# A hybrid attention and DeltaNet backbone: the emission order waits for small transfers, row loads move into the last column block, and scale-and-shift steps choose their engine

## The chip, the core and the metric

The kernel runs on one core of a Trainium2 chip. The metric is the device time of one execution in microseconds: 1731.31 us, the median of three runs (1731.27 to 1731.7). The engines are TensorE (PE in the profile; its weight loads are PEld), VectorE (DVE), ScalarE (ACT), GpSimd (POOL) and SyncE (SP), which issues nearly all transfers.

## What is computed

Two layers act on 256 latent tokens and 256 context tokens of width 2048. Per layer and stream:

```
h  = layernorm(x) * (1 + scale) + shift          # scale, shift, gate = silu(c) @ w_mod + b_mod
p  = h @ w_in                                    # 2048 x 6672: q, k, v, gates of three head groups
ya = attention(qa, ka, va) * silu(za)            # group A: 8 query heads on 2 key heads; rmsnorm and rotary on q, k
yb = window_attention(qb, kb, vb, bias) * silu(zb)   # group B: 4 heads, learned 2-D bias
yc = rmsnorm(gated_deltanet(conv(qkv))) * silu(zc)   # group C: 4 heads, forward and backward scans over chunks
y  = concat(ya, yb, yc) @ w_out                  # 2048 x 2048
x  = layernorm(ALPHA * x + gate * y) * ln_g + ln_b
```

Latent tokens also attend to the context's keys, and the scans start from the context's states. In the second layer the context serves only keys, values and states; its queries, gates and output are left out, so those items of `w_in` run on the latent columns alone. The output is the latent stream.

## The kernel before

**Tiling.** Everything is fp32. Activations lie transposed (features on the partitions) in 16 tiles of 128 features, 512 tokens wide (context in columns 0 to 255). Each fp32 product is three matmuls in a reduced format: the weight and the activation are each split into a high and a low part (`wHL` from `raw`; `hH`, `hL` or `hv`). Splitting a weight piece of 128x512 costs a copy (`high`, on ScalarE or VectorE) and a subtraction on VectorE. One item of `w_in` makes 128 output features and is four such pieces, accumulated in one PSUM bank of ring `mm` (two banks). The output projection goes by column blocks `nb` of 512 and over 16 feature tiles `k` in `K_ORDER`; `ki` counts them.

**Order of the work.** The program plans its own instruction order (class `Order`, L102). It keeps an estimated time for each engine; every emitted operation moves its engine's time on by a cost formula, and a transfer is taken to land 2.0 us after its issue (0.75 us on SP, 1.0 on POOL). Side work is written as Python generators, the tasks. A task yields when it would have to wait; `poll` (L185), called between matmuls, resumes those whose time has come on PE's estimated clock and stops when VectorE or ScalarE are planned 2.5 or 3.5 us ahead of PE. A plain `yield` waits until what the task has issued so far should be done, `yield 0` until the next poll, and `yield ("at", t)` until the planned time t. `until` (L201) moves PE's planned time forward until a condition holds. The engines then run each its own instructions strictly in this order, and wait for real semaphores.

**Buffers.** A `Ring` (L215) hands out the buffers of one size: `tmp` has five, `cin` fifteen, `yq` eighteen, `wr` sixteen; `get` waits for one to be free at the planned time.

**The pieces that the change touches.** `mod_dve` (L650) computes part of the second layer's modulation on VectorE, beside the first layer's projections: eight times it broadcasts 256 values to a tile `xsb` by two transfers on SP, then multiplies rows with it. `ln_scale` gives mean and scale of rows; `normalise` (L753) applies them to a 128x512 piece, by turns on ScalarE and VectorE. `h_run` (L786) transposes the normalised rows and applies scale and shift, by turns too. `gates` (L885) prepares the scan's decays. `ev_ka` (L1003) and `ev_qa` (L1050) take a key or query projection out of PSUM, with squares `sq`, the rotary's temporary `t2` and, in the second layer, the result `q` in `tmp` buffers. `ev_qb` (L1119) does it for group B and loads the head's bias table `tbm` (one buffer) from POOL. `run_wo` (L1735) is the output projection; at `ki` 2 of each column block it spawns `ep_load`, which loads the gate row and two residual pieces for that block (three transfers of 256 KB).

**The norm between the layers.** When the last column block of 256 rows is out of PSUM, `finish` (L1845) normalises the rows in four pieces, multiplies by `ln_g`, adds `ln_b`, normalises once more for the next layer and runs `h_all`, which gives the next layer's activations. It goes in steps: step s normalises piece s, multiplies piece s-1, adds to piece s-2 and takes statistics of piece s-3. The rows of gamma and beta (`lg`, `lb`) are broadcast to 128 partitions, one pair of 256 KB transfers per piece. The latent rows (s = 1) finish first, during the context's column blocks; the context rows (s = 0) finish while PE runs the second layer's first six items, which need latent columns alone. The first item after them needs both streams. Before, `finish` itself spawns the loads, three pairs at once:

```
while nb > at_nb[0] + 2:
    yield 0.3
...
od.resume(od.spawn(loads()))
sc = yield from ln_scale(st, "lnp")
```

The last layer's end has its own function, `finish_last`, which the change leaves alone.

Of the kernel before, what the change touches and what calls it, by code (L numbers as in the profile page):

```python
# [10 lines left out]
ALU = mybir.AluOpType  # L11
# [33 lines left out]

N_FIRST, LATE = 6, 3
ROPE_V = 0

# [166 lines left out]
class Ring:  # L215
# [18 lines left out]
    def get(self, name, **k):  # L234
        while True:
# [4 lines left out]
            else:  # L240
                return self.take(name, **k)

    def put(self, n=1, t=None):
        o = self.order
        if t is None:
            t = max(o.last.values()) if o.last else 0.0
        self.times += [t] * n
        assert len(self.times) <= self.n, f"ring {self.tag}"


class Flag:
# [6 lines left out]
    def get(self):  # L258
        while not self.free:
            yield self  # L260


# [120 lines left out]
def hybrid_grid_flow(  # L383
# [266 lines left out]
    def mod_dve(l, groups):  # L650
# [30 lines left out]
        for k0 in range(0, DM, 256):  # L681
            xb = big.tile([128, 2, 256], F32, tag="xsb", bufs=1, name="xsb")
            for r in range(2):
                rows = xsd[r * KT + k0 // 128:r * KT + k0 // 128 + 2, :]
                Q.dma_start(xb[:, r], rows.rearrange("(o a) b -> o (a b)", o=1).to_broadcast([128, 256]))
            yield
            for g, f, s in todo:
                while od.wr[raw_key(ready[0])][1] > od.t["PE"]:
                    yield 0.3
                t = ready.pop(0)  # L690
                for r in range(2):
                    due += pace
                    while od.t["DVE"] > od.t["PE"] + DVE_LAG and od.t["PE"] < due:
                        yield 0.3
                    m = modT[l][:, s, r, f:f + 1]
                    V.tensor_tensor_reduce(
                        out=t if r else junk, in0=t, in1=xb[:, r], scale=1.0, op0=ALU.mult, op1=ALU.add, accum_out=m,
                        scalar=m if k0 else bmt[l][:, s, f:f + 1])
                    yield 0
                load()  # L700
                if k0 + 256 == DM and s and f + 1 == sum(g):
                    mod_ok[l, g].set()
# [47 lines left out]

    turn = [0]

    def normalise(p, sc):  # L753

        turn[0] ^= 1
        if turn[0]:
            S.activation(p, p, AF.Identity, scale=sc[0], bias=sc[1])
        else:
            V.tensor_scalar(p, p, sc[0], sc[1], op0=ALU.mult, op1=ALU.add)

# [25 lines left out]
    def h_run(l, streams, xn, ab_ps, wab):  # L786
# [9 lines left out]
        def turn():  # L796
            kts, pt, ring = flying.pop(0)
            hf = yield from cin.get("hf")
            for i, (kt, s) in enumerate([(kt, s) for kt in kts for s in streams]):
                c = slice(i * 256, i * 256 + 256)  # L800
                if kts[0] // n % 2:
                    V.tensor_scalar(hf[:, c], pt[:, c], mt[:, 1, s, kt:kt + 1], mt[:, 0, s, kt:kt + 1],
                                    op0=ALU.mult, op1=ALU.add)
                else:
                    S.activation(hf[:, c], pt[:, c], AF.Identity, scale=mt[:, 1, s, kt:kt + 1],
                                 bias=mt[:, 0, s, kt:kt + 1])
            ring.put()
# [77 lines left out]
    def gates(l, ab_ps):  # L885
# [50 lines left out]
        V.tensor_scalar(g.neg_G, g.G[:, 0:32], -1.0, None, op0=ALU.mult)  # L936
        yield
        p4 = yield from tr.get("gT")
        T.transpose(p4[0:32, 0:128], g.G[:, 0:32], ident)
# [3 lines left out]
        yield  # L943
        gt = (yield from tmp.get("gt"))[0:32, 0:128]
        V.tensor_copy(gt, p4[0:32, 0:128])
# [57 lines left out]
    def ev_ka(l, lo, ps, ring, h):  # L1003
        nrm = L[l]["nrm"]
        sq = yield from tmp.get("ksq")
        S.activation(sq, ps, AF.Square)
        k = yield from yq.get("ka")
        t2 = yield from tmp.get("krt")
        S.activation(k[:, 0:256], ps[:, 0:256], AF.Copy, scale=nrm[:, 1:2])
        yield from rope(k[:, 256:512], ps, L[l]["tabk"], t2[:, 0:256])  # L1010
        ring.put()
        tmp.put()
        yield
        r = yield from tmp.get("kr")
        pb = yield from at.get("kss")
# [34 lines left out]
    def ev_qa(l, lo, ps, ring, h):  # L1050
        nrm = L[l]["nrm"]
        sq = yield from tmp.get("qsq")
        S.activation(sq[:, lo:], ps[:, lo:], AF.Square)
        two = SPLIT(l, "a")
        q = yield from (tmp if two else yq).get("qa")
        t2 = yield from tmp.get("qrt")
        if lo == 0:
# [61 lines left out]
    def ev_qb(l, lo, ps, ring, h):  # L1119
# [11 lines left out]
        t6 = tbm.rearrange("p (a b) -> p a b", a=6)  # L1131
        G.dma_start(tbm, tb[l, :, h])
        V.tensor_tensor(t6, t6, bc(namask, 6), op=ALU.add)
        yield
# [600 lines left out]
    def run_wo(it):  # L1735
# [13 lines left out]
        if ki == 2:  # L1749
            for s in ss:  # L1750
                od.spawn(ep_load(l, s, nb))
        if ki == 8 and nb == 2 and l == DEPTH - 1:
            od.spawn(load_gb(l))
# [90 lines left out]

    def finish(l, s, rp, st):  # L1845
        gb, at_nb = {}, [0]

        def loads():
            for nb in range(4):
                while nb > at_nb[0] + 2:  # L1850
                    yield 0.3
# [6 lines left out]

        od.resume(od.spawn(loads()))
        sc = yield from ln_scale(st, "lnp")  # L1860
        st2 = [bn_tile() for _ in range(2)]

        for step in range(7):
# [4 lines left out]
            if 0 <= nb < 4:  # L1868
                while nb not in gb:
                    yield 0.3  # L1870
                for i in range(2):
                    V.tensor_tensor(rp[i][nb], rp[i][nb], gb[nb][0], op=ALU.mult)
# [240 lines left out]
```

## Time and profile before

| | before |
|---|---|
| median of 3 runs | 1731.31 us (1731.27 to 1731.7) |
| the profiled execution | 1732.42 us |
| its span, first to last instruction | 1730.6 us |
| TensorE busy | 1657.6 us (96%) |
| VectorE busy | 1321.0 us (76%) |
| ScalarE busy | 852.9 us (49%) |
| mean granted TensorE clock | 0.990 |
| moved by DMA | 296.3 MB, 171 GB/s on average |

Busy times are shares of the span over stages with different limits. Line L348 in the rows is the helper through which every VectorE, ScalarE, POOL and SP instruction is recorded, L367 and L377 those of matmul and transpose, so instructions are told apart by the tiles that they write and read.

### The profile page before, as it was taken

To read this page: it belongs to the slowest core of one execution; us is meant where nothing else is said; L and a number is where in the kernel's file an instruction comes from. 1 tells how busy PE (TensorE), PEld (TensorE's weight loads), DVE (VectorE), ACT (ScalarE), POOL (GpSimd) and SP (SyncE) were. 2 spreads that over 40 slices of the span, in tenths; PEclk is the share of its full clock that TensorE was granted. 3 is DMA by queue.
4 is the path that set the end of the run, shared out by engine and by line. 5 is a ranking of instruction groups with operands and counts; after the bars stand their busy time and mean duration, and the time that the engine had idled before them with its cause. 6 is when DMAs were issued, how large, how long until landed. Compare 5 with 4: busy or idle time off the path is not lost. (4 is left out here: it accounts for less than half of the span.)

```text
span 1730.6 us, 30951 instructions
## 1 busy us (share of the span) xinstructions
PE 1657.6 (96%) x10527; PEld 1338.1 (77%) x10527; DVE 1321.0 (76%) x3973; ACT 852.9 (49%) x1939; POOL 43.0 (2%) x112
## 2 busy tenths in 40 slices
PE   4999999999999999999999898999999999999996
PEld 1667778787777788878788777777898888888785
DVE  5345888888878788878897797768788778675667
ACT  2225556454444544455534464555565654554543
POOL 0000100000001000000000000000000000000000
PEclk9999999999999999999999999999999999999998
DMA  9993544544554546444567866345454544444475
GB/s 322 340 355 108 161 132 121 179 141 140 159 180 138 170 144 191 141 137 132 152 211 247 261 216 208 103 125 150 122 159 149 161 117 132 113 142 135 145 228 181
DMA packets 213486, 296.32 MB, mean 171 GB/s; under 512 B 38384, under 2 KB 104656, under 8 KB 213328
## 3 DMA queue, kind: packets, MB, share of 16 engines
q1 hardware_dynamic: 211632, 291.07, 54.7%
q0 software_dynamic: 1696, 3.27, 0.7%
q8 instruction: 83, 1.36, 0.3%
q14 instruction: 75, 0.61, 0.1%
HBM read 287.88 MB, written 6.37 MB: 170 GB/s over the span
## 5 line engine op out<-in xcount | busy, mean ns | idle before, releaser
L367 PE MATMUL acc<-hH,wHL 128*128 128x512 f32 x1664 | 573.9, 407 | 0.7 <-ACT hH L348 0.5
L348 DVE TENSOR_TENSOR wHL<-raw,wHL 128x512 fp32r<-128x512 f32 (+1 forms) x600 | 396.3, 671 | 84.9 <-ACT wHL L348 67.0
L367 PE MATMUL acc<-hv,wHL 128*128 128x256 f32 (+1 forms) x2496 | 448.1, 332 | 10.3 <-DVE wHL L348 7.2
L367 PEld LDWEIGHTS acc<-hv,wHL 128*128 128x128 f32 x2496 | 369.4, 192 | 63.2 <-DVE wHL L348 9.3
L348 ACT ACTIVATE wHL<-raw 128x512 fp32r<-128x512 f32 (+1 forms) x511 | 302.7, 610 | 222.2 <-PE o L367 64.2
L367 PEld LDWEIGHTS acc<-hH,wHL 128*128 128x128 f32 x1664 | 312.5, 188 | 85.0 <-issue 18.2
L367 PE MATMUL acc<-hL,wHL 128*128 128x512 f32 x832 | 324.9, 390 | 0.2 <-DVE hL L348 0.2
L367 PE MATMUL o<-wHL,hv 128*128 128x512 f32 x1092 | 259.1, 396 | 9.5 <-DVE hv L348 3.7
L367 PEld LDWEIGHTS o<-wHL,hv 128*128 128x128 f32 x1092 | 206.4, 191 | 58.2 <-DVE hv L348 4.4
L367 PEld LDWEIGHTS acc<-hL,wHL 128*128 128x128 f32 x832 | 156.8, 189 | 30.6 <-issue 3.6
L348 DVE CUSTOM_DVE_ANT_0 gvj<-gvl,xsb,modT 128x256 f32<-128x256 f32 x224 | 107.5, 480 | 13.5 <-DMA xsb<-xsd 9.6
L348 DVE CUSTOM_DVE_ANT_0 gvl<-gvl,xsb,modT 128x256 f32<-128x256 f32 x224 | 108.2, 483 | 8.4 <-DMA xsb<-xsd 2.7
L367 PE MATMUL md<-gvr,xs 128*32 128x128 f32 (+1 forms) x1408 | 88.8, 349 | 24.4 <-DMA gvr<-in_w_mod_dram 23.6
L367 PEld LDWEIGHTS md<-gvr,xs 128*32 128x32 f32 x1408 | 32.9, 113 | 65.7 <-issue 30.6
L348 ACT ACTIVATE P<-P,zz 128x512 f32<-128x512 f32 (+1 forms) x60 | 38.1, 656 | 81.0 <-DVE zz L348 78.3
L348 DVE TENSOR_TENSOR R<-R,Xt 128x60 f32<-128x60 f32 (+24 forms) x248 | 53.5, 216 | 9.1
L348 DVE TENSOR_TENSOR Xt<-X,R 128x60 f32<-128x60 f32 (+24 forms) x248 | 52.2, 211 | 4.5 <-ACT X L348 0.2
L367 PE MATMUL pv<-PT,v 128*128 128x128 f32 (+1 forms) x288 | 52.6, 298 | 1.4 <-ACT PT L348 1.4
L348 DVE SCALAR_TENSOR_TENSOR cv<-acc,cw,cv 128x510 f32<-128x510 f32 (+1 forms) x48 | 33.8, 704 | 20.7 <-ACT cv L348 19.8
L367 PEld LDWEIGHTS pv<-PT,v 128*128 128x128 f32 x288 | 42.3, 191 | 6.0 <-ACT PT L348 1.9
L348 DVE TENSOR_REDUCE mx<-sc 128x1 f32<-128x512 f32 (+1 forms) x60 | 41.3, 688 | 5.3 <-PE sc L367 4.5
L348 ACT ACTIVATE PT<-ptr 128x512 f32<-128x512 f32 (+1 forms) x55 | 32.7, 594 | 20.1 <-PE ptr L377 19.6
(306 smaller groups left out, 1904.7 us busy)
## 6 DMA issues: line engine op xcount, KB each, us to landing
raw<-in_w_in_dram SPq DMA_DIRECT2D x398, 256.0 KB
gvr<-in_w_mod_dram SPq DMA_DIRECT2D x256, 256.0 KB
raw<-in_w_out_dram SPq DMA_DIRECT2D x176, 256.0 KB
gvl<-in_w_modt_dram SPq DMA_DIRECT2D x256, 128.0 KB
raw<-in_w_in_dram SPq DMA_DIRECT2D x36, 128.0 KB
xp<-in_xin_dram SPq DMA_DIRECT2D x16, 256.0 KB
E<-growd SPq DMA_DIRECT2D x16, 256.0 KB
xres<-in_xin_dram SPq DMA_DIRECT2D x16, 256.0 KB
```

What stands on the lines that cost most here:

```text
L348: r = fn(*a, **k)
L367: r = self.real.matmul(out, lhsT, rhs, **k)
```

## The change

`LANDING` is 1.5. After a transfer to a small tile, three places now wait in the plan until 1.5 us after its planned landing before they emit the instruction that reads it: `xsb` in `mod_dve`, `tbm` in `ev_qb`, and `lb` in `finish`. The loads of `lg` and `lb` become a function `gb_load`, which `run_wo` calls in the last column block of the first layer at `ki` 3; it keeps at most two pairs ahead of the adds instead of three. `normalise` and `h_run` choose the engine whose planned time is earlier (`affine`). `ev_ka` and `ev_qa` take all their `tmp` buffers together (`some`), and `ev_ka` reuses one. `gates` takes its `tmp` buffer before the transpose's PSUM bank.

```diff
+LANDING = 1.5
 class Ring:
+    def some(self, *names):
+        n = len(names)
+        while True:
+            if len(self.times) < n:
+                yield Many(self, n)
+            elif sorted(self.times)[n - 1] > self.order.t["PE"]:
+                yield ("at", sorted(self.times)[n - 1])
+            else:
+                return [self.take(x) for x in names]
+class Many(Flag):            # free when the ring has n buffers
+    ...
 def mod_dve(l, groups):
-            yield
+            yield ("at", od.wr[raw_key(xb)][1] + LANDING)
+    def affine(dst, src, mul, add):
+        if max(od.t["DVE"], od.t["PE"]) + HIGH_BIAS < max(od.t["ACT"], od.t["PE"]):
+            V.tensor_scalar(dst, src, mul, add, op0=ALU.mult, op1=ALU.add)
+        else:
+            S.activation(dst, src, AF.Identity, scale=mul, bias=add)
     def normalise(p, sc):
-        turn[0] ^= 1
-        if turn[0]:
-            S.activation(p, p, AF.Identity, scale=sc[0], bias=sc[1])
-        else:
-            V.tensor_scalar(p, p, sc[0], sc[1], op0=ALU.mult, op1=ALU.add)
+        affine(p, p, sc[0], sc[1])
 def h_run ... turn():
-                if kts[0] // n % 2:
-                    V.tensor_scalar(hf[:, c], pt[:, c], ...)
-                else:
-                    S.activation(hf[:, c], pt[:, c], AF.Identity, ...)
+                affine(hf[:, c], pt[:, c], mt[:, 1, s, kt:kt + 1], mt[:, 0, s, kt:kt + 1])
 def gates(l, ab_ps):
+        gt = (yield from tmp.get("gt"))[0:32, 0:128]
         p4 = yield from tr.get("gT")
...
-        gt = (yield from tmp.get("gt"))[0:32, 0:128]
 def ev_ka(l, lo, ps, ring, h):
-        sq = yield from tmp.get("ksq")
-        S.activation(sq, ps, AF.Square)
         k = yield from yq.get("ka")
-        t2 = yield from tmp.get("krt")
+        sq, t2 = yield from tmp.some("ksq", "krt")
+        S.activation(sq, ps, AF.Square)
...
-        tmp.put()
         yield
-        r = yield from tmp.get("kr")
+        r = t2
 def ev_qa(l, lo, ps, ring, h):
-        sq = yield from tmp.get("qsq")
+        two = SPLIT(l, "a")
+        if two:
+            sq, t2, q = yield from tmp.some("qsq", "qrt", "qa")
+        else:
+            q = yield from yq.get("qa")
+            sq, t2 = yield from tmp.some("qsq", "qrt")
         S.activation(sq[:, lo:], ps[:, lo:], AF.Square)
-        two = SPLIT(l, "a")
-        q = yield from (tmp if two else yq).get("qa")
-        t2 = yield from tmp.get("qrt")
 def ev_qb(l, lo, ps, ring, h):
         G.dma_start(tbm, tb[l, :, h])
+        yield ("at", od.wr[raw_key(tbm)][1] + LANDING)
         V.tensor_tensor(t6, t6, bc(namask, 6), op=ALU.add)
 def run_wo(it):
+        if ki == 3 and nb == 3 and l == 0:
+            gb_load(l, ss[0])
-    def finish(l, s, rp, st):
-        gb, at_nb = {}, [0]
+    gbs = {}
+    def gb_load(l, s):
+        gb, at_nb = gbs[s] = {}, [0]
         def loads():
             for nb in range(4):
-                while nb > at_nb[0] + 2:
+                while nb > at_nb[0] + 1:
                     yield 0.3
...
-        od.resume(od.spawn(loads()))
+        od.spawn(loads())
+    def finish(l, s, rp, st):
+        gb, at_nb = gbs[s]
         sc = yield from ln_scale(st, "lnp")
...
                 while nb not in gb:
                     yield 0.3
+                yield ("at", od.wr[raw_key(gb[nb][1])][1] + LANDING)
```

## Rows read from the trace of the kernel before

**Rows 1.** The page, parts 1 and 2: busy us of each engine; granted clock by slices.
```profile
PE 1657.6 (96%) x10527; PEld 1338.1 (77%) x10527; DVE 1321.0 (76%) x3973; ACT 852.9 (49%) x1939; POOL 43.0 (2%) x112
...
PEclk9999999999999999999999999999999999999998
```
**Rows 2.** Windows: stretch, then PE, PEld, DVE, ACT, POOL, clock, DMA share, GB/s.
```profile
0.00:130.00 130.00, 104.51 (x1113) 61.78 (x1114) 57.24 (x148) 35.05 (x74) 3.00 (x9) 1.00 1.03 339
```
**Rows 3.** Timeline of SP's issues at the latent rows' norm: start, us, instruction, count.
```profile
965.01 0.43 SPq L348 DMA_DIRECT2D gatep<-gscr  x1
...
969.48 0.39 SPq L348 DMA_DIRECT2D lb<-in_ln_b_dram  x1
970.20 4.58 SPq L348 DMA_DIRECT2D raw<-in_w_out_dram  x5
```
**Rows 4.** Timeline there, ScalarE, PE and VectorE; in brackets the idle time before.
```profile
979.50 3.25 ACT L348 ACTIVATE wHL<-raw 128x512 fp32r<-128x512 f32 x5 [5.59 <-DMA raw<-in_w_out_dram]
...
980.18 1.22 PE L367 MATMUL o<-wHL,hv 128*128 128x512 f32 x2 [2.71 <-ACT wHL L348]
...
987.07 1.30 DVE L348 TENSOR_TENSOR res<-res,lg 128x512 f32<-128x512 f32 x2 [3.46 <-DMA lg<-in_ln_g_dram]
...
991.42 1.88 PE L367 MATMUL o<-wHL,hv 128*128 128x512 f32 x7 [1.48 <-DVE wHL L348]
```
**Rows 5.** Windows of the same stretch.
```profile
975.00:980.00 5.00, 2.47 (x11) 1.70 (x10) 5.00 (x10) 0.50 (x1) 0.00 (x0) 1.00 1.00 356
980.00:985.00 5.00, 4.35 (x9) 2.98 (x10) 3.62 (x7) 3.24 (x6) 0.00 (x0) 0.50 0.90 275
985.00:990.00 5.00, 4.94 (x18) 3.62 (x16) 2.93 (x5) 1.78 (x3) 0.00 (x0) 0.82 1.02 337
990.00:1000.00 10.00, 8.58 (x38) 7.11 (x39) 10.00 (x18) 3.60 (x6) 0.00 (x0) 1.00 0.80 251
```
**Rows 6.** PE's groups from 1043 to 1092 (busy, mean, idle), and its timeline after.
```profile
L367 PE MATMUL acc<-hv,wHL 128*128 128x256 f32 x288 | 39.4, 299 | 7.4 <-DVE wHL L348 5.0 <-ACT wHL L348 2.2 <-DVE gy L348 0.2
...
1093.52 0.33 PE L377 MATMUL htr<-cst,res 128*128 128x128 f32 x1 [2.17 <-ACT res L348]
```
**Rows 7.** Timeline of VectorE and SP at the context rows' norm.
```profile
1057.84 1.38 DVE L348 TENSOR_TENSOR wHL<-raw,wHL 128x512 fp32r<-128x512 f32 x2 [3.07 <-ACT wHL L348]
...
1060.89 1.29 DVE L348 TENSOR_TENSOR res<-res,lb 128x512 f32<-128x512 f32 x2
...
1068.71 0.42 SPq L348 DMA_DIRECT2D lg<-in_ln_g_dram  x1
...
1074.69 1.29 DVE L348 TENSOR_TENSOR res<-res,lg 128x512 f32<-128x512 f32 x2 [3.58 <-DMA lg<-in_ln_g_dram]
```
**Rows 8.** Timeline of SP and VectorE at an `xsb`; PE's waits from 130 on.
```profile
478.72 0.90 SPq L348 DMA_DIRECT2D xsb<-xsd  x2
...
483.52 0.49 DVE L348 CUSTOM_DVE_ANT_0 gvj<-gvl,xsb,modT 128x256 f32<-128x256 f32 x1 [3.69 <-DMA xsb<-xsd]
...
PE scan L367 <- DVE rr L348: 3.0, 2, 1.6
```
**Rows 9.** Timeline of VectorE and PE at the last bias table.
```profile
1620.81 0.56 DVE L348 TENSOR_TENSOR tbm<-tbm,cst 128x384 f32<-128x384 f32 x1 [4.92 <-DMA tbm<-in_tb_dram]
...
1623.57 0.73 PE L367 MATMUL o<-wHL,hv 128*128 128x512 f32 x2 [3.69 <-DVE hv L348]
...
1644.72 3.48 PE L367 MATMUL o<-wHL,hv 128*128 128x512 f32 x8 [0.96 <-ACT hv L348]
```
**Rows 10.** Instructions on tile res, 960 to 1100: ns min, median, max.
```profile
L348 ACT ACTIVATE res<-res,lnpnm,lnpy x8: 797/802/817, 971.0 to 1063.4; 128x512 f32<-128x512 f32 x8
L348 DVE TENSOR_SCALAR res<-res,lnpy,lnpnm x8: 365/542/549, 971.5 to 1064.8; 128x512 f32<-128x512 f32 x8
```
**Rows 11.** PE's waits from 130 us on: total us, times, longest.
```profile
PE sc L367 <- DVE HL L348: 3.0, 1, 3.0
...
PE acc L367 <- ACT qrt L348: 0.6, 1, 0.6
```

More of the change, by code (lines that the diff above doesn't have):

```diff
@@ L260, in get, with __init__, free @@
             yield self
+class Many(Flag):
+    def __init__(self, ring, n):
+        self.ring, self.n = ring, n
+    @property
+    def free(self):
+        return self.ring.free >= self.n
 class Want(Flag):
@@ L749, in ln_scale @@
         return [(r[:, i:i + 1], nm[:, i:i + 1], mv[:, i, 0:1]) for i in range(m)]
-    turn = [0]
-    def normalise(p, sc):
-        turn[0] ^= 1
-        if turn[0]:
-            S.activation(p, p, AF.Identity, scale=sc[0], bias=sc[1])
-        else:
-            V.tensor_scalar(p, p, sc[0], sc[1], op0=ALU.mult, op1=ALU.add)
+    def affine(dst, src, mul, add):
[3 more added lines that the diff above has]
+            S.activation(dst, src, AF.Identity, scale=mul, bias=add)
+    def normalise(p, sc):
+        affine(p, p, sc[0], sc[1])
     def ln_finish(tiles, sts, name):
@@ L800, in turn @@
                 c = slice(i * 256, i * 256 + 256)
-                if kts[0] // n % 2:
-                    V.tensor_scalar(hf[:, c], pt[:, c], mt[:, 1, s, kt:kt + 1], mt[:, 0, s, kt:kt + 1],
-                                    op0=ALU.mult, op1=ALU.add)
-                else:
-                    S.activation(hf[:, c], pt[:, c], AF.Identity, scale=mt[:, 1, s, kt:kt + 1],
-                                 bias=mt[:, 0, s, kt:kt + 1])
+                affine(hf[:, c], pt[:, c], mt[:, 1, s, kt:kt + 1], mt[:, 0, s, kt:kt + 1])
             ring.put()
@@ L1004, in ev_ka @@
         nrm = L[l]["nrm"]
-        sq = yield from tmp.get("ksq")
+        k = yield from yq.get("ka")
+        sq, t2 = yield from tmp.some("ksq", "krt")
         S.activation(sq, ps, AF.Square)
-        k = yield from yq.get("ka")
-        t2 = yield from tmp.get("krt")
         S.activation(k[:, 0:256], ps[:, 0:256], AF.Copy, scale=nrm[:, 1:2])
```

## The prediction

> **What bounds the kernel now.** I read the page first. TensorE is busy 1657.6 of 1730.6 us, so all the idle that any reordering could remove is 73.0 us, and the strip of the granted clock shows it near full level almost everywhere [rows 1]. Next the stretches: the first 130 us hold 130 - 104.5 = 25.5 us of that idle, with the DMA engines saturated at 339 GB/s [rows 2]; no edit moves a byte there. That leaves 47.5 us. What ends those gaps I then took from the waits of PE and from timelines. They are few and local, and most lie where a late transfer held VectorE or ScalarE, whose later work PE needed. So the sum is made gap by gap, not from busy shares.
>
> The profiled execution took 1732.4 us (span 1730.6 and 1.8 around it); the median of the runs is 1731.3, 1.1 lower. I sum against 1732.4 and shift the end by -1.1.
>
> **Part A, the first norm (latent rows, 965 to 992 us).** Before, `finish` issues six 256 KB row loads at the moment when the next column block issues its three: nine transfers go out on SP from 965.0 to 969.9, ahead of the first weight load at 970.2 [rows 3]. The reader sees ScalarE wait 5.59 us for weights, then PE idle 2.71 us [rows 4]. The DMA moved 356 GB/s meanwhile, so this is backlog, not latency [rows 5]. PE then ran at the lower level, 1.2 GHz: granted 0.50 over 5 us and 0.82 over the next 5, a loss of 2.5 + 0.9 = 3.4 us [rows 5]. Later VectorE stood 3.46 us for the last gamma, with PE's next weights behind it: 1.48 us more [rows 4]. Together 2.71 + 1.48 + 3.4 = 7.6 us.
>
> The change issues two of the four pairs (four transfers) one matmul group after the block's own three, in the last block, where PE still has 12 groups to run. It makes a burst of seven instead of nine there, and leaves three at the norm. Each transfer is 0.26 MB, or 0.74 us at 356 GB/s, so seven cost 1.5 us less backlog than nine: I leave 2.71 - 1.5 = 1.2 us of PE idle, too short to bring the lower clock by the rows here (the 1.48 us gap ends at 991.4 and the clock stays at 1.00 after it). Gain 7.6 - 1.2 = 6.4; I take 6.0, since the last pair is still issued late and the plan's 3.5 us for its landing is shorter than the 6.0 measured in part B. Bounds: 7.6 if the moved burst is free, 0 if it makes the same gap and clock loss earlier.
>
> **Part B, the second norm (context rows, 1043 to 1097 us).** PE runs six latent-only items (288 matmuls in 39.4 us, with 7.4 us of idle among them) and then needs the context rows' output: it waits 2.17 us before 1093.5 [rows 6]. So removing the 7.4 us does nothing by itself: PE would arrive earlier and wait longer. The length of `finish` decides. Before: the second add ends at 1062.2; the load of the last pair, which it releases, is issued at 1068.71 and lands at 1074.69, 12.5 us after the add (6.5 in SP's queue behind weight loads, 6.0 in transfer); from there to the first transpose are 18.8 us [rows 7]. After: the 3.07 us stall of VectorE behind late weights [rows 7] goes with the burst, so the add ends at 1059.1. But only two pairs are ahead now, so `finish` meets two such waits in series (third and fourth pair), with a multiply and an add of 1.3 us each between them. Its end is 1059.1 + w1 + 2.6 + w2 + 18.8 = 1080.5 + W, against 1093.5: even at W = 13.0. The code's own floor for one wait is 1.5 for two issues + 2.0 + LANDING 1.5 = 5.0 us; the row's ceiling is 12.5. I take 6.5, the measured transfer plus one issue of 0.43, because VectorE no longer stands in front of the weight loads' buffers. W = 13: no change, between -3.0 and +12.0. The moved burst costs its 1.2 us here as well (at about 1022). B = +1.2, from -1.8 to +13.2.
>
> The Trainium skill, DMA: Bandwidth & Descriptors, section on the anatomy of one DMA, gives a fixed 2.0 us plus bytes over 436 GB/s; an estimate from it for 256 KB is 2.6 us, under the 3.5 us that the plan now allows. By it W is at the floor of 10 and B is -1.8, the sum 3.0 us better. The trace disagrees here, 6.0 us for this transfer under load, so VectorE may still stand some 2.5 us each time.
>
> **Part C, the eight `xsb` broadcasts.** A plain `yield` already waits 2.1 us in the plan; the new one waits 3.5. The longest stall, 3.69 us, ended 3.9 us after its issue was done at 478.72 + 0.90, and held the scan's `rr` that PE needed [rows 8]. PE's two gaps behind `rr` are 3.0 us in all [rows 8]. With 1.4 us later emission the stalls shrink by 1.4 each: 1.36 goes, 1.62 becomes 0.2. C = -2.8, from -3.0 to 0. Eight later starts of 1.4 us are 11 us on a task that is paced by a due time; its end is covered by the whole output projection.
>
> **Part D, the eight bias tables.** One of eight stalls VectorE: 4.92 us at 1620.8, with PE idle 3.69 us behind the `hv` queued there [rows 9]. After, VectorE does `wHL` and `hv` first. But this head is the last of the layer, and the projection waits for its result: 0.96 us at 1644.7 [rows 9]. The table lands no earlier, so the head ends no earlier, and most of the 3.69 moves there. D = -1.0, from -4.6 to +1.0. The other seven tables wait for their buffer and are long there; 3.5 us on their heads lies beside projections.
>
> **Part E, engine choice, buffers taken together, order in `gates`.** A normalise costs 0.80 us on ScalarE and 0.54 on VectorE [rows 10]; eight per norm pass split evenly. Moving all four of VectorE's to ScalarE would free 2.2 us on VectorE for 3.2 on ScalarE, which has half its time free [rows 1]; the same choice in `h_run` and in the first layer's start costs as little, and there the DMA hides it [rows 2]. `some` removes waits made while holding buffers, and `ev_ka` takes one buffer less; the gap that PE shows behind such a projection is 0.6 us, the one before a query's scores 3.0 us [rows 11]. Each reorder also shifts everything after it. E = 0, from -4 to +4; the gaps of row size 0.5 to 3.0 which it could remove or make give that size. `gt` taken earlier only frees a PSUM bank: 0.
>
> **Sum:** -6.0 + 1.2 - 2.8 - 1.0 + 0 = -8.6; 1732.4 - 8.6 = 1723.8, less 1.1 gives 1722.7: I predict **1723 us**.
>
> **The rivals.**
> 1. *The gain is taken back (0.22).* The waits stay, only later: W = 20 instead of 13 (+7), or the moved burst makes its gap in the last block. For it: PE already waits for `finish`, and the last attention head is late. Against: the largest term, A, has no such partner; the latent norm has the whole context projection behind it. 1722.7 + 7 = 1730; at the ceiling W = 25 it is 1735.
> 2. *Slower: three temporary buffers at once (0.18).* Place: the eight query heads of the second layer. `ev_qa` now needs three of five `tmp` buffers free together, while single takers pass it; meanwhile it holds one of two PSUM accumulators. PE's cover is one item, 39.4 / 6 = 6.6 us. Each us beyond it is PE idle: 2 us on each of eight heads is +16, so 1739. It decides from 8.6 / 8 = 1.1 us beyond the cover. For it: five buffers for six kinds of user. Against: only 0.6 us of PE's idle lies there now, and a task that holds none lets the others finish.
> 3. *More (0.12).* W = 10 (-3.0), the 3.0 us before a query's scores go too, and D gains 3 more because the last head ends earlier: 1722.7 - 9 = 1714. For it: VectorE, late at each of these places, is relieved at all of them. Against: every one needs its own luck.
> 4. *The change doesn't do what it says.* Transfers land later than the plan's 3.5 us (6.0 above), so the stalls only shrink; this is counted inside rival 1.
>
> **How the numbers follow.** 0.2% of 1731 is 3.5 us, about what a measurement here can tell from no change: same means 1727.8 to 1734.8. The forecast has 0.48, its own range 1717 to 1729 (faster 0.44, same 0.04). Rival 1 gives 0.05 faster, 0.14 same, 0.03 slower; rival 2 0.03 same and 0.15 slower; rival 3 0.12 faster. Faster 0.61, same 0.21, slower 0.18. The range that leaves out some 2 in 10 reaches from just under rival 3 to just above the ceiling of rival 1: 1712 to 1736.
>
> **What would show it.** A: no PE gap over 1.5 us between 965 and 992 and a clock of 1.00 there; seven transfers on SP early in the last block. B: PE's idle gathers in one stretch before the first context transposes, VectorE waits little for `lg`; two separate pairs of issues. C: no `xsb` wait over 2.5 us. D: no gap at the `hv` there, a longer one at the projection's 15th group. Wrong, if the stretch from 1043 to 1097 grows by over 10 us, if PE shows waits behind `qrt` or for an accumulator over 5 us in all, or if the clock falls in the last block.

## The result and the profile after

| | before | after |
|---|---|---|
| median | 1731.51 us (1731.27 to 1736.57, 4 runs) | 1715.28 us (1714.17 to 1716.87, 4 runs) |
| the profiled execution, its span | 1732.42, 1730.6 us | 1715.62, 1713.8 us |

The ratio is 0.9898 (95%: 0.9885 to 0.9912): 16.2 us less. 8.6 were forecast. The sign and the range (1712 to 1736) held, the size did not.

The page of after, parts 1 and 2, beside [rows 1]:

```profile
PE 1652.3 (96%) x10527; PEld 1335.7 (78%) x10527; DVE 1306.7 (76%) x3953; ACT 861.5 (50%) x1959; POOL 42.9 (3%) x112
...
PEclk9999999999999999999999999999999999999999
```

PE does the same 10527 matmuls; its idle time fell from 73.0 to 61.5 us, and its busy time by 5.3, while the mean granted clock rose from 0.990 to 0.993. To find where, I cut both traces at three marks in PE's timeline:

| stretch of PE's timeline | before | after | change | forecast |
|---|---|---|---|---|
| start to the first `o<-wHL,hv` (first layer's output projection) | 853.4 | 849.1 | -4.3 | -2.8 (C) |
| to the first `acc<-hv,wHL` 128x256 (second layer, latent columns) | 189.8 | 185.3 | -4.5 | -4.8 (A with its moved burst) |
| to the first `acc<-hv,wHL` 128x512 (the context rows' norm) | 54.2 | 49.2 | -5.0 | 0 (B) |
| to the end | 633.3 | 630.2 | -3.1 | -1.0 (D) |

In after, eight matmuls of an attention head (`ptr` and `pv`, about 1 us) come behind the first mark instead of ahead of it, so the first row shows about 1 us too much gain and the second as much too little. With that the rows of C and A came out within 1 us of their forecasts. B, taken as even, is the largest miss. The last row is not D's alone: three kernels without D's wait (only_norm, norm_wait and norm_move, below) are 2.0 to 2.2 us shorter there too.

**A.** Windows of after at the latent rows' norm (PE, PEld, DVE, ACT, POOL, clock, DMA share, GB/s), beside [rows 5]. PE is busy throughout, the clock is at 1.00, the 2.4 GHz level, where [rows 5] had 0.50 and 0.82:

```profile
975.00:980.00 5.00, 5.00 (x24) 4.14 (x23) 4.69 (x9) 2.96 (x6) 0.00 (x0) 1.00 0.79 201
...
985.00:990.00 5.00, 5.00 (x24) 4.14 (x23) 4.92 (x9) 2.23 (x4) 0.00 (x0) 1.00 0.98 266
```

The third pair of rows, whose load SP issues at 974.32, holds VectorE up for only 0.31 us; SP and VectorE of after there:

```profile
974.32 0.42 SPq L369 DMA_DIRECT2D lg<-in_ln_g_dram  x1
...
978.62 1.29 DVE L369 TENSOR_TENSOR res<-res,lg 128x512 f32<-128x512 f32 x2 [0.31 <-DMA lg<-in_ln_g_dram]
```

**B.** VectorE of after at the context rows' norm, beside [rows 7]: the first add, the third multiply, the second add, a split that waited for ScalarE, the fourth multiply, the second normalise.

```profile
1048.40 1.29 DVE L369 TENSOR_TENSOR res<-res,lb 128x512 f32<-128x512 f32 x2
...
1055.02 1.28 DVE L369 TENSOR_TENSOR res<-res,lg 128x512 f32<-128x512 f32 x2
1056.22 1.29 DVE L369 TENSOR_TENSOR res<-res,lb 128x512 f32<-128x512 f32 x2
...
1065.31 0.69 DVE L369 TENSOR_TENSOR wHL<-raw,wHL 128x512 fp32r<-128x512 f32 x1 [2.30 <-ACT wHL L369]
1065.92 1.29 DVE L369 TENSOR_TENSOR res<-res,lg 128x512 f32<-128x512 f32 x2
...
1078.52 1.92 DVE L369 TENSOR_SCALAR res<-res,ln1y,ln1nm 128x512 f32<-128x512 f32 x4
```

The first add ends at 1048.40 + 1.29 = 1049.7 and the third multiply starts 5.3 later; the second add ends at 1057.5 and the fourth starts 8.4 later. W = 13.7; the forecast was 13.0. VectorE never stands before a gamma row; 2.30 of w2 are a wait for ScalarE's half of a split. But from the fourth multiply to the second normalise are 12.6 us, where before has 1091.10 - 1074.69 = 16.4. PE of after, beside [rows 6]: its idle time is now in one stretch, as forecast.

```profile
1073.25 1.46 PE L388 MATMUL acc<-hv,wHL 128*128 128x256 f32 x10 [1.29 <-DVE wHL L369]
1079.38 0.48 PE L398 MATMUL htr<-cst,res 128*128 128x128 f32 x1 [4.68 <-ACT res L369]
1080.79 1.54 PE L398 MATMUL htr<-cst,res 128*128 128x128 f32 x6 [0.93 <-ACT res L369]
```

**D.** PE of after at the second layer's last head, beside [rows 9]. The 3.69 us gap before `o<-hv` is gone, the wait of the projection for that head stayed, and a gap before a transpose came:

```profile
1625.87 0.66 PE L398 MATMUL ptr<-cst,P 128*128 128x128 f32 x4 [1.41 <-DVE PTL L369]
...
1629.64 2.82 PE L388 MATMUL o<-wHL,hv 128*128 128x512 f32 x6 [0.97 <-ACT hv L369]
```

### The profile page after: what moved, and what is told of

Same layout as the page of the kernel before. It is cut to its first block, busy times and chain, and to the rows that moved or that the text cites. A ratio compares the mean times of both kernels' runs of the same rounds, so it can differ in the third digit from the quotient of the medians.

```text
span 1713.8 us, 30928 instructions
## 1 busy us (share of the span) xinstructions
PE 1652.3 (96%) x10527; PEld 1335.7 (78%) x10527; DVE 1306.7 (76%) x3953; ACT 861.5 (50%) x1959; POOL 42.9 (3%) x112
## 4 chain that ended last, share of the span: by engine, by line
PE 76%; DMA 9%; DVE 9%; ACT 3%; issue 2%; SPq 1%; DVEq 0%; ACTq 0%
PE acc L388 49%; PE o L388 11%; DMA gvr<-in_w_mod_dram 6%; PE scan L388 3%; DVE wHL L369 2%; PE pv L388 2%; PE md L388 2%; PE sc L388 2%; DMA raw<-in_w_out_dram 2%; PE lv L388 1%; PE ptr L398 1%; DVE res L369 1%; DMA xsb<-xsd 1%; DVE gvl L369 1%; DMA lg<-in_ln_g_dram 1%
## 5 line engine op out<-in xcount | busy, mean ns | idle before, releaser
L388 PE MATMUL acc<-hv,wHL 128*128 128x256 f32 (+1 forms) x2496 | 443.2, 331 | 5.8 <-DVE wHL L369 4.6
L388 PEld LDWEIGHTS acc<-hL,wHL 128*128 128x128 f32 x832 | 157.1, 189 | 30.5 <-issue 3.8
L369 ACT ACTIVATE hf<-htr,modT 128x256 f32<-128x256 f32 x62 | 31.7, 562 | 38.5 <-PE htr L398 38.3
```

The costliest lines, as they stand in the source:

```text
L369: r = fn(*a, **k)
L388: r = self.real.matmul(out, lhsT, rhs, **k)
```

## The experiments

Theory 1: the gain is the stalls at the two norms. Rival 2: half of it is the choice of engine. Rival 3: it is scatter of the new order. Later, Theory 2: the `xsb` waits matter only together with other parts, at one place. Medians; "change" is against before on the same chip, with the ratio's interval. Before moved from 1731.5 to 1735.6 between chips, so kernels of different groups compare to about 3 us.

| kernel | median us | change | ratio, 95% |
|---|---|---|---|
| only_norm | 1717.84 | -14.3 | 0.9902 to 0.9935 |
| only_affine | 1740.49 | +8.3 | 1.0029 to 1.0069 |
| only_some | 1740.81 | +8.6 | 1.0034 to 1.0074 |
| only_waits | 1733.22 | +1.1 | 0.9988 to 1.0023 |
| norm_wait | 1724.74 | -7.3 | 0.9940 to 0.9975 |
| norm_move | 1724.16 | -7.9 | 0.9940 to 0.9974 |
| no_norm | 1725.27 | -6.8 | 0.9956 to 0.9983 |
| no_waits | 1730.71 | -1.3 | 0.9981 to 1.0005 |
| no_xsb | 1722.47 | -9.0 | 0.9932 to 0.9963 |
| affine_xsb | 1730.74 | -0.8 | 0.9970 to 1.0003 |
| late_add | 1715.48 | -16.0 | 0.9887 to 0.9923 |
| ahead3 | 1707.81 | -23.7 | 0.9846 to 0.9879 |
| no_tbm | 1721.14 | -14.5 | 0.9908 to 0.9945 |
| no_affine | 1713.37 | -22.2 | 0.9860 to 0.9894 |
| no_some | 1712.48 | -23.1 | 0.9852 to 0.9896 |
| ahead4 | 1707.16 | -28.4 | 0.9825 to 0.9865 |

### The four parts, each alone

**only_norm**: before with `gb_load` in the last column block, two pairs ahead, and the landing wait in `finish`.

```diff
+        if ki == 3 and nb == 3 and l == 0:
+            gb_load(l, ss[0])
-                while nb > at_nb[0] + 2:
+                while nb > at_nb[0] + 1:
+                yield ("at", od.wr[raw_key(gb[nb][1])][1] + LANDING)
```

> The kernel before with the norm edit alone: row loads moved into the last column block, two pairs ahead, and the wait for their landing. Theory 1 (the gain is the stalls at the two norms): the first output projection starts within 1 us of before, it ends 4.5 us earlier, and the stretch from the first latent-only item to the first two-stream item shrinks from 54.2 to about 49 us; in all -9.5 us, 1722. Rival 2 (the engine choice carried half of it): -5, 1726, with the stretch at 52 us or more. Rival 3 (scatter of the reordering): any value from -4 to +4 in stretches that the edit does not touch.

**only_affine**: before with `affine` in `normalise` and `h_run`.

```diff
+        if max(od.t["DVE"], od.t["PE"]) + HIGH_BIAS < max(od.t["ACT"], od.t["PE"]):
+            V.tensor_scalar(dst, src, mul, add, op0=ALU.mult, op1=ALU.add)
+        else:
+            S.activation(dst, src, AF.Identity, scale=mul, bias=add)
```

> The kernel before with the engine choice alone (normalise and h_run take the engine whose planned time is earlier). Theory 1: between -2 and +1 us, the stretch of the context norm stays at 53 to 54 us. Rival 2: -4 to -6 us, and that stretch shrinks by 3 us or more, since VectorE gives work away there. Rival 3: -4 to +4, spread over stretches without a norm.

**only_some**: before with `some` in `ev_ka` and `ev_qa`, and the earlier `gt`.

```diff
+        sq, t2 = yield from tmp.some("ksq", "krt")
+            sq, t2, q = yield from tmp.some("qsq", "qrt", "qa")
```

> The kernel before with the buffers alone (key and query projections take all their temporary buffers together; gates takes its buffer before the PSUM bank). Theory 1: 0, within 1.5 us. Rival 2: 0. Rival 3: -4 to +4, with PE's gaps of 0.5 to 3 us at other places than before.

**only_waits**: before with the waits for `xsb` and `tbm`.

```diff
+            yield ("at", od.wr[raw_key(xb)][1] + LANDING)
+        yield ("at", od.wr[raw_key(tbm)][1] + LANDING)
```

> The kernel before with the two small waits alone (the broadcast rows of mod_dve and the bias tables of the second head group). Theory 1: -4 us from the first 853 us (two gaps behind rr of 1.62 and 1.36 us) and -3 in the last layer (the 3.69 us gap at hv), 1724. Rival 2: the same. Rival 3: less than -2, since the places refill.

The norm edit alone gives 14.3 us, half as much again as expected. Rival 2 falls: engine choice alone makes the kernel slower. The four do not add: -14.3 + 8.3 + 8.6 + 1.1 is +3.7, together they give -16.2. Both slow kernels lose at one place, the change from the first layer's projections to its output projection. There the last DeltaNet head's output must be scaled (`c_osc`, on VectorE and ScalarE) before PE can transpose it. VectorE, ScalarE and PE of only_affine:

```profile
855.25 0.48 DVE L348 CUSTOM_DVE_ANT_0 gvj<-gvl,xsb,modT 128x256 f32<-128x256 f32 x1 [2.00 <-DMA xsb<-xsd]
...
857.44 0.48 DVE L348 CUSTOM_DVE_ANT_0 gvl<-gvl,xsb,modT 128x256 f32<-128x256 f32 x1 [1.70 <-DMA xsb<-xsd]
...
860.32 0.15 DVE L348 TENSOR_TENSOR ort<-ory 128x4 f32<-128x4 f32 x1
...
861.10 0.16 DVE L348 TENSOR_TENSOR c_osc<-ory,c_rqd 128x4 f32<-128x4 f32 x1
...
861.30 1.28 ACT L348 ACTIVATE o<-O,c_osc 128x128 f32<-128x128 f32 x4 [7.18 <-DVE c_osc L348]
...
861.76 1.35 PE L377 MATMUL otr<-cst,o 128*128 128x128 f32 x4 [6.45 <-ACT o L348]
```

VectorE stands 2.00 and 1.70 us before two `xsb` tiles and then has their multiplications to do; the small `ort` and `c_osc` are queued behind. ScalarE idles 7.18 us, PE 6.45, and PE then runs at the lower clock. Windows of only_affine:

```profile
860.00:865.00 5.00, 3.24 (x9) 2.47 (x10) 4.75 (x21) 3.70 (x11) 0.00 (x0) 0.50 0.29 91
865.00:870.00 5.00, 5.00 (x19) 4.01 (x18) 4.89 (x18) 2.50 (x8) 0.00 (x0) 0.80 0.51 147
```

only_some has the same picture (PE idle 5.86). In after that scale came 18 us sooner, before the projections ended, and PE does not wait for it:

```profile
843.54 1.26 ACT L369 ACTIVATE o<-O,c_osc 128x128 f32<-128x128 f32 x4
```

### The norm edit in halves, and two parts taken out

**norm_wait**: before with the landing wait alone. **norm_move**: before with the moved loads, two pairs ahead, alone.

```diff
 norm_wait
+                yield ("at", od.wr[raw_key(gb[nb][1])][1] + LANDING)
 norm_move
+        if ki == 3 and nb == 3 and l == 0:
+            gb_load(l, ss[0])
-                while nb > at_nb[0] + 2:
+                while nb > at_nb[0] + 1:
```

> The kernel before with one half of the norm edit: the adds wait in the plan for the landing, the loads stay where they were (three pairs at once, when the norm starts). Theory 1 (two places, two causes): the burst of nine transfers at 965 to 970 stays, and with it PE's 2.7 us gap and the lower clock of the output projection, so little of the 4.5 us there is won; at the context rows' norm VectorE no longer stands before a gamma row, so the splits queued behind it are emitted first and the stretch from the first context-free item to the first context item shrinks from 54 to about 49 us. In all -4 to -8 us against before. Rival (the early loads do it all): within 2 us of before. Rival (the wait alone does it all): -12 to -14.

> The kernel before with the other half: loads issued in the last column block and two pairs ahead, and no landing wait. Theory 1: the gaps of 975 to 992 and the lower clock go (-5 to -6 us there); at the context rows' norm only two pairs are ahead, so VectorE stands in its order before the third and fourth gamma row, 3 to 5 us each, and the stretch stays at 54 or grows to 58. In all -6 to 0 against before. Rival (the early loads do it all): -12 to -14, the stretch 48 us.

**no_norm**: after without the norm edit. **no_waits**: after without the `xsb` and `tbm` waits.

```diff
 no_norm
-            gb_load(l, ss[0])
...
-                yield ("at", od.wr[raw_key(gb[nb][1])][1] + LANDING)
 no_waits
-            yield ("at", od.wr[raw_key(xb)][1] + LANDING)
-        yield ("at", od.wr[raw_key(tbm)][1] + LANDING)
```

> The changed kernel without the norm edit (engine choice, buffers taken together and the xsb and tbm waits against before). If the single parts added, +8 (engine choice) + 9 (buffers) + 1 (waits) = +18, 1750 us. If the loss of the two is one gap at the last DeltaNet head of the first layer, which the xsb waits take away because VectorE then doesn't stand before that head's scale, it is near or under before: 1725 to 1732. By what the norm edit gave alone (14.3) it should be 1715.3 + 14.3 = 1729.6.

> The changed kernel without the xsb and tbm waits. Alone these waits gave +1.1 (nothing). Theory 2 (the xsb wait protects the last DeltaNet head once the other parts have moved it): the 6 us gap of PE before the first output transposes at 850 to 860 is back with its lower clock, and the time is 1722 to 1730. Rival (that gap was the accident of each part alone, the waits are worth nothing): 1714 to 1718, no gap over 2 us at 845 to 865.

The halves add here: -7.3 and -7.9 against -14.3. (The trace of norm_wait is of its fastest execution, 1720.36, and shows more than its median; 3.1 us of its gain lie ahead of the output projection, where its instructions are those of the kernel before.) They work in different places, and the other way round than I expected: of norm_wait I expected little at A and a stretch of 49 us at B, of norm_move 5 to 6 us less at A and a stretch of 54 us or more at B. The projection takes 184.4 us in norm_wait and 189.6 in norm_move, the stretch of B 52.4 and 49.5. In norm_move the burst at the column block is three transfers, as in after, and yet the projection is as long as in the kernel before. VectorE and PE of norm_move:

```profile
983.13 1.29 DVE L349 TENSOR_TENSOR res<-res,lg 128x512 f32<-128x512 f32 x2 [2.12 <-DMA lg<-in_ln_g_dram]
...
992.51 1.29 DVE L349 TENSOR_TENSOR res<-res,lg 128x512 f32<-128x512 f32 x2 [2.69 <-DMA lg<-in_ln_g_dram]
...
987.48 7.36 PE L368 MATMUL o<-wHL,hv 128*128 128x512 f32 x24 [2.16 <-DVE wHL L349]
996.85 3.50 PE L368 MATMUL o<-wHL,hv 128*128 128x512 f32 x10 [2.02 <-DVE wHL L349]
```

VectorE stands before two gamma rows, and the weight splits behind it make PE wait 2.16 and 2.02 us; the granted clock is 0.80 to 0.86 from 985 to 1005. norm_wait issues all nine transfers at once, as in [rows 3], from 961.89 to 966.98. Its SP (the first of the six rows' transfers, the first weights behind them), its ScalarE and its PE:

```profile
963.31 0.43 SPq L349 DMA_DIRECT2D lg<-in_ln_g_dram  x1
...
967.08 1.23 SPq L349 DMA_DIRECT2D raw<-in_w_out_dram  x1
...
974.54 3.23 ACT L349 ACTIVATE wHL<-raw 128x512 fp32r<-128x512 f32 x5 [3.76 <-DMA raw<-in_w_out_dram]
...
975.22 6.47 PE L368 MATMUL o<-wHL,hv 128*128 128x512 f32 x26 [0.87 <-ACT wHL L349]
982.15 8.23 PE L368 MATMUL o<-wHL,hv 128*128 128x512 f32 x35 [0.46 <-DVE wHL L349]
```

So at A two such stalls, without the burst, cost what before loses, and the landing wait takes them away. All 18 traces agree: the output projection takes 183.9 to 187.5 us in the eleven kernels with the wait in `finish` and 189.6 to 195.2 in the seven without it, norm_move among them. What the burst cost beside the stall is not shown. Until the first weights behind the burst land, PE, VectorE and ScalarE run the same instructions in the same order in norm_wait and in the kernel before, and so does SP up to the fifth of these weight loads. Yet the weights released ScalarE 7.5 us after their issue in norm_wait (967.08 to 974.54), against 9.3 us before the change (970.20 to 979.50, [rows 3] and [rows 4]). The difference is as large as that between PE's gaps, 2.71 and 0.87 us, so the edit did not make it. And norm_move trades the burst for late loads: with two pairs ahead the third and fourth go out only at 978.28 and 984.80. No kernel moves the loads with three pairs ahead and without the wait.

At B, one row of windows for each kernel: from the fourth multiply to the second normalise, with the weight splits (`wHL`) that VectorE does inside it: length, busy (count). Before:

```profile
1074.69:1091.10 16.41, 6.50 (x10) 0.90 0.48 155
```

norm_move:

```profile
1071.43:1086.75 15.32, 5.91 (x9) 0.89 0.56 174
```

norm_wait:

```profile
1069.51:1082.11 12.60, 3.30 (x6) 0.99 0.56 170
```

After:

```profile
1065.92:1078.52 12.60, 3.32 (x6) 0.95 0.49 143
```

Where VectorE stands before the row, ten or nine splits are left for this window. Where the plan waits instead, VectorE does part of them first, and six are left, one of them begun before it: 3.2 of the 3.8 us. From the first to the second normalise VectorE starts 19 splits in both kernels; nine of them come ahead of the fourth multiply in before, 14 in after. The landing wait hardly shortens the norm by itself, since the multiply then comes later. Here is VectorE from its first to its second normalise: length, busy (count). Before:

```profile
1052.58:1091.10 38.52, 30.77 (x61) 0.91 0.65 210
```

norm_move:

```profile
1052.91:1086.75 33.84, 31.00 (x62) 0.95 0.71 221
```

norm_wait:

```profile
1044.14:1082.11 37.97, 31.46 (x63) 0.95 0.71 225
```

After:

```profile
1043.93:1078.52 34.59, 30.49 (x62) 0.98 0.74 229
```

VectorE's work is nearly the same in all four; the lengths differ by its idle time, 7.8, 2.8, 6.5 and 4.1 us. norm_wait still issues six row loads when the norm starts, and VectorE waits 3.56 us at 1048.70 for weights that go out after them; with the moved loads that wait is gone. So most of the gain at B comes with the moved loads, and only_norm, with both halves, has 47.7 us there.

no_waits shows Theory 2's gap again, with the `xsb` stalls ahead of it. VectorE and PE of no_waits:

```profile
850.63 0.49 DVE L369 CUSTOM_DVE_ANT_0 gvj<-gvl,xsb,modT 128x256 f32<-128x256 f32 x1 [1.49 <-DMA xsb<-xsd]
...
853.22 0.48 DVE L369 CUSTOM_DVE_ANT_0 gvl<-gvl,xsb,modT 128x256 f32<-128x256 f32 x1 [2.09 <-DMA xsb<-xsd]
...
857.53 1.35 PE L398 MATMUL otr<-cst,o 128*128 128x128 f32 x4 [6.33 <-ACT o L369]
```

The waits are worth 1730.71 - 1715.28 = 15.4 us in the changed kernel and nothing alone. no_norm fits Theory 2 (1725 to 1732) and not the sum of parts (1750): it has the two parts that lose 8 us each alone, and the waits, and no gap over 1 us at that place. The norm edit is worth 1725.27 - 1715.28 = 10.0 us in the changed kernel, less than the 14.3 alone.

### The waits one by one, a longer wait, more pairs ahead

**no_xsb**: after without the `xsb` wait. **affine_xsb**: before with `affine` and the `xsb` wait. **late_add**: 3.0 us more in `finish`. **ahead3**: three pairs ahead.

```diff
 no_xsb
-            yield ("at", od.wr[raw_key(xb)][1] + LANDING)
 affine_xsb
+            yield ("at", od.wr[raw_key(xb)][1] + LANDING)
+        affine(p, p, sc[0], sc[1])
 late_add
-                yield ("at", od.wr[raw_key(gb[nb][1])][1] + LANDING)
+                yield ("at", od.wr[raw_key(gb[nb][1])][1] + LANDING + 3.0)
 ahead3
-                while nb > at_nb[0] + 1:
+                while nb > at_nb[0] + 2:
```

> The changed kernel without the xsb waits alone (the tbm wait stays). Theory 2 (the xsb wait keeps VectorE free for the last DeltaNet head of the first layer): PE's gap of about 6 us before the first output transposes at 850 to 860 is back with its lower clock, 1724 to 1728. Rival (the 15 us that both waits were worth came from tbm or from scatter): 1714 to 1719 and no such gap.

> The kernel before with engine choice and the xsb waits. Engine choice alone took 1740.5 and had PE idle 6.5 us at 855, behind a scale that VectorE reached late because it stood before an xsb tile. Theory 2: that gap is gone, the first product of the first layer's output projection comes at 850 us or earlier instead of 863, and the time is 1726 to 1733. Rival (engine choice is slower in itself): 1737 to 1742.

> The changed kernel with 3.0 us more in the landing wait of finish alone (4.5 instead of 1.5). If finish is the path at the context rows' norm, the third and the fourth multiply are emitted up to 3 us later each, the stretch from the first latent-only item to the first context item grows from 49.2 to 52 to 55 us, and the time by 3 to 6: 1718 to 1721. If PE has cover there, or the plan's wait is already longer than it says, within 1 us of 1715.3.

> The changed kernel with three pairs of rows ahead of the adds instead of two (all six transfers issued in the last column block). Theory 1: one wait in series goes at the context rows' norm, so the last multiply comes about 17.5 us after the first normalise instead of 22.0, PE's gap of 4.7 us before the first context transpose and the lower clock behind it shrink, and the time is 1709 to 1713. Rival (a burst of nine in the last column block costs what it cost at 965 in the kernel before): a gap of 1 to 3 us at 943 to 955 with a lower clock, and 1715 to 1720.

affine_xsb bears Theory 2 out: against only_affine the gap is gone and 9 us with it (+8.3 became -0.8); the first product of the output projection comes at 851.5, not at 850 or earlier as expected, against 862.8. ScalarE of affine_xsb, without an idle time in front:

```profile
850.05 1.28 ACT L349 ACTIVATE o<-O,c_osc 128x128 f32<-128x128 f32 x4
```

no_xsb loses 7.2 us, and PE idles 5.1 us at that place, but by another route than I expected: the DeltaNet scale is early (842.46); late is an attention head's reciprocal `zz`, which VectorE reaches behind a run of `xsb` multiplications. PE of no_xsb:

```profile
850.48 0.66 PE L398 MATMUL ptr<-cst,P 128*128 128x128 f32 x4 [2.26 <-ACT P L369]
853.96 1.11 PE L398 MATMUL otr<-cst,o 128*128 128x128 f32 x4 [2.82 <-ACT PT L369]
```

late_add: the stretch of B grew from 49.2 to 51.7 us, the low end of what was expected, and PE's gap with it. The median stayed within 0.2 us of after; a price under 3 us can't be told from none across chips, so its size stays open. PE of late_add:

```profile
1082.76 0.47 PE L398 MATMUL htr<-cst,res 128*128 128x128 f32 x1 [8.83 <-ACT res L369]
```

ahead3 is faster than both kernels: 1707.8. One wait in series is gone; the fourth multiply comes 14.2 us after the first normalise (1045.15) instead of 22.0, the stretch of B takes 42.7 us instead of 49.2. VectorE and PE of ahead3; the rival's burst costs one gap of 0.87:

```profile
1052.97 1.28 DVE L369 TENSOR_TENSOR res<-res,lg 128x512 f32<-128x512 f32 x2
...
1059.30 1.29 DVE L369 TENSOR_TENSOR res<-res,lg 128x512 f32<-128x512 f32 x2
...
1074.66 1.91 DVE L369 TENSOR_SCALAR res<-res,ln1y,ln1nm 128x512 f32<-128x512 f32 x4
...
955.35 0.73 PE L388 MATMUL o<-wHL,hv 128*128 128x512 f32 x2 [0.87 <-ACT wHL L369]
...
1075.71 0.98 PE L398 MATMUL htr<-cst,res 128*128 128x128 f32 x7 [0.75 <-DVE res L369]
1077.62 1.03 PE L398 MATMUL htr<-cst,res 128*128 128x128 f32 x4 [0.93 <-DVE hf L369]
```

### The size of D, what E is worth inside, all pairs ahead

**no_tbm**, **no_affine**, **no_some**: after without that part. **ahead4**: four pairs ahead.

```diff
 no_tbm
-        yield ("at", od.wr[raw_key(tbm)][1] + LANDING)
 no_affine
-        affine(p, p, sc[0], sc[1])
+        turn[0] ^= 1
 no_some
-        sq, t2 = yield from tmp.some("ksq", "krt")
+        sq = yield from tmp.get("ksq")
 ahead4
-                while nb > at_nb[0] + 1:
+                while nb > at_nb[0] + 3:
```

> The changed kernel without the tbm wait alone. Term D said -1.0. By the traces so far the stretch from the end of the second layer's projections to its held groups is 77.1 us with the wait and 79.0 to 79.6 without, so PE's gap of 3.7 us before o<-hv is back and the time is 1717 to 1719. Rival (the difference of 8 us between the changed kernel without both waits and without the xsb wait alone is all tbm): 1722 to 1725. Rival (nothing): 1714.5 to 1716.

> The changed kernel with turns instead of engine choice. Alone, engine choice made the kernel 8 us slower through one gap, which the xsb waits took away. If it is worth nothing once that gap is closed, 1714 to 1718. If its own cost of 8 us is still in the changed kernel, 1706 to 1709. If it earns there what the changed kernel has over the norm edit alone, 1718 to 1722.

> The changed kernel with temporary buffers taken one by one as before (and the gates' buffer after the PSUM bank). Worth nothing once the gap at the last DeltaNet head is closed: 1714 to 1718. Own cost of 8 us still there: 1706 to 1709. A gain from it: 1718 to 1722, with a gap behind qrt or before a query's scores that the changed kernel does not have.

> The changed kernel with all four pairs of rows ahead (eight transfers in the last column block, eleven with the block's own three). With three ahead it took 1707.8 and PE's gaps before the first context transposes were down to 0.75 and 0.93. If the second wait in series still sets that end, the last multiply comes some 3 us earlier and 1 to 2 us go: 1705.5 to 1707. If PE's own work is the bound now, no change: 1707 to 1709. If the burst of eleven delays the weights of the last column block, a gap over 2 us at 943 to 960 and 1710 to 1713.

no_tbm: the stall at the last head is back, 4.56 us on VectorE and 3.34 on PE.

```profile
1610.80 0.56 DVE L369 TENSOR_TENSOR tbm<-tbm,cst 128x384 f32<-128x384 f32 x1 [4.56 <-DMA tbm<-in_tb_dram]
...
851.87 1.75 PE L388 MATMUL pv<-PT,v 128*128 128x256 f32 x4 [1.80 <-ACT PT L369]
...
1613.55 1.22 PE L388 MATMUL o<-wHL,hv 128*128 128x512 f32 x2 [3.34 <-DVE hv L369]
```

But the time rose by 5.9 (4.8 by the ratios), and in the trace 5.0 of it was there by 854: the DeltaNet scale is back at 851.79, where before has it (852.00), and PE idles 1.80 us there. The stretch to the end is 2.0 us longer than in after (632.3 against 630.2), so at the last head itself the wait is worth some 2 us. The first layer's tables show no stall; the wait acts there through the order alone.

no_affine and no_some are 1.9 and 2.8 us under after, by the ratios 3.6 and 4.1; the intervals just overlap. So engine choice and buffers earn nothing here and may cost up to 4; the 8 us that each loses alone go with the gap at 850 to 862, which after doesn't have. ahead4 is no better than ahead3 by more than scatter. From the first to the second normalise VectorE idles 0.2 of 29.5 us in ahead3 and 0.2 of 30.0 in ahead4, so the waits in series no longer set the end.

## Why the prediction was wrong in size

**A (-4.8 forecast with its burst, -4.5 measured): the number held, its split among causes did not.** I split 7.6 us into a burst of nine transfers and a stalled VectorE, and put most of it on the burst. norm_move has no burst there and wins nothing: its two stalls before gamma cost as much as burst and stall together did. The signs I named held: seven transfers in the last block, no gap over 1.5 us, clock 1.00. They could not tell the causes apart. How much the burst cost beside the stall stays open. PE's gap behind it is 0.87 us in norm_wait, 2.71 in before and 2.97 in no_norm, though norm_wait and the kernel before run the same instructions up to it.

**B (0 forecast, -5.0 measured): the step that failed.** "From there to the first transpose are 18.8 us" was carried over behind W, as if VectorE did none of this work during W. (The add that releases the last pair in before, which ends at 1062.2, is the first, not the second; the sum does not change by it.) W was right, 13.7 against 13.0. But that stretch of before held the splits that had piled up while VectorE stood before the row, and W, now spent in the plan and not in VectorE's queue, is time in which VectorE does them: I counted them twice. 16.4 became 12.6, and the 18.8 became 1079.38 - 1065.92 = 13.5. ScalarE, which before came to its half of the normalise only at 1092.66, starts it together with VectorE: 1.2 us more up to the first context item. The sum to make was VectorE's work plus its idle time: 30.8 + 7.8 us before, 30.5 + 4.1 after. The estimate from the Trainium skill (DMA: Bandwidth & Descriptors, the anatomy of one DMA, a fit for transfers that GpSimd issues), 2.6 us for such a transfer, would have put W at 10; here a row's pair that SP issued at 974.32 released VectorE at 978.62, 4.3 us, and W was not at its floor.

**C (-2.8) and D (-1.0): no terms of their own.** The stalls shrank as worked out: in after the longest wait for `xsb` is 1.83 us, and PE no longer waits for `rr` [rows 8]. D's path was wrong, though: most of the 3.69 us was to move to the wait of the projection for the last head, and that is 0.97 us, as before (0.96). Alone the two waits gave nothing (only_waits); inside the changed kernel they give 15.4, no_xsb 7.2 and no_tbm 5.9. What decides is whether VectorE reaches the last heads' small operations before PE has run out of projections. I looked for a stall's own cover and not for what else is queued at that junction.

**E (0, from -4 to +4): 0 inside, outside its bounds alone.** The bounds came from gaps that PE had; +8.3 and +8.6 came from a gap it did not have, 6 us and the lower clock after it.

**The rivals.** Rival 3 (1714) is nearest in time, but not by its routes: W is not 10, and the 3.0 us before a query's scores is still there (2.96 at 1189.9). Rival 2's wait for three buffers is nowhere in the waits of after. Rival 1, the gain taken back, has nothing for it.

## What to carry to other kernels

When a wait moves from an engine's queue into the plan, work out again what follows it: what had piled up behind the wait is now done during it. In a kernel with a planned order, price an edit by where PE changes from one kind of work to the next; there the small operations of the last heads decide, and parts that cost 8 us alone can be free together. Where one engine sets a stretch, add its work and its idle time instead of waits and pieces in series. Before splitting a gain among causes, look for the row that only one of them would leave: here VectorE waits 2.1 to 5.2 us for gamma in each of the seven kernels with the long projection, and at most 1.1 in the others. And see whether two traces already differ where they run the same instructions.

## Not expected of the hardware

Executions of one program differ by as much as most of the effects under test: before took 1725.76 to 1740.45 us in 13 runs on one chip, no_norm 1723.49 to 1731.07 in ten, while after stayed within 1714.17 to 1716.87 in four. Such a 256 KB row landed 6.0 us after its issue in [rows 7] and 4.3 in after, and the first weights behind the same nine transfers released ScalarE after 9.3 us in before and 7.5 in norm_wait. What makes them vary is not shown.
